# One decoder layer on one core: the output projection of the token mixer by seven half-size products instead of eight blocks

## The chip, the cores and the metric

One core of a Trainium2 chip. A core has a matrix engine (TensorE, PE in the profile, with its weight loads as PEld), three engines for elementwise work (VectorE or DVE, ScalarE or ACT, GpSimd or POOL), a queue engine for transfers (SyncE or SP), an on-chip memory SBUF, and eight PSUM banks of 128 x 512 fp32 in which matmuls add up. Every engine runs its own instructions in their order in the program; waits between engines are semaphores. The metric is the device time of one execution in microseconds (us), lower is better.

## The reference, cut to what matters

A layer is a gated linear attention (GLA) mixer and a gated feed-forward part with a convolution, each on an RMS-normed input and added to the residual x, and a last norm. x is 1024 tokens by 1024 features, fp32.

```python
def gla_mixer(x, w_in, w_alpha_up, b_alpha, out_norm, w_out):
    proj = x @ w_in
    q, k, v, r, a_low = jnp.split(proj, ...)
...
    _, o = lax.scan(step, state0, (qc, kc, vc, cum))    # 4 heads, chunks of 64 tokens
    o = rms_norm(o, out_norm.reshape(h, dv)).reshape(b, s, GLA_DV)
    return (o.astype(x.dtype) * jax.nn.silu(r)) @ w_out
...
def conv_ffn(x, w_up, conv_w, conv_b, w_down):
    u = x @ w_up                                        # 1024 -> 2 * 2816
    u = sum(u_pad[:, j:j + s] * conv_w[j] for j in range(CONV_WIDTH)) + conv_b
    gate, up = jnp.split(u, 2, axis=-1)
    return (jax.nn.silu(gate) * up) @ w_down
...
    x = x + mixer(rms_norm(x, norm1))
    x = x + conv_ffn(rms_norm(x, norm2), ...)
    return rms_norm(x, final_norm)
```

The change is in the last line of `gla_mixer`: g = norm(o) * silu(r), a 1024 x 1024 matrix, times `w_out`, 1024 x 1024.

## The kernel before, in words

Every fp32 product is made of three matmuls on numbers split in two (hi is the value cast to fp32r, lo is the rest): hi times hi, hi times lo, lo times hi (`mm3`, lines 96, 98, 100; `prod`, line 560). A split is an ACT cast (hi) and a DVE subtraction (lo): lines 86 and 87 for a unit of weights (128 x 1024), 517 and 518 for g, 618 and 619 for the normed x.

The stages, in the order of PE's work: the projections q, k, v and the GLA chain head by head (chain matmuls `s_ps`, `u_ps`, `o_ps`; DVE and ACT work between them, lines 425 to 465); then r, in two column halves c = 0, 1 of eight token blocks of 128 each (`r_ps`, 24 matmuls of 128 x 512 per block); after each block silu (`sr`), the gate product g (`og`, POOL line 505, DVE line 511), four transposes of g (`gt_ps`) and its split into the big tile T. The last head's GLA chain runs beside the first blocks of r. Then the output projection (`out_tok`, tile `o_ps2`, which the profile shows as `o_ps`): two column halves n of eight token blocks of 24 matmuls, added by DVE to x (tiles `x2a` for tokens 0 to 511 and `x2b` for the rest, line 580). During n = 1, `norm2(tok)` squares and norms each finished token block (ACT `x2n`, `junk`; POOL `rstd`; DVE line 589) and `feat(tok - 2)` transposes it (`t_ps`, 8 transposes), splits it into T and, for the second half of the tokens, forms the sums that the feed-forward part's Strassen scheme needs (`combine`: lines 600 to 603 on DVE, with POOL's `r` additions of line 552). Last come the first two (plain) feature blocks of the feed-forward part (`plain_mm`, tile `u_ps`) and then its Strassen products (`xb`, `yb`, `zb`).

A scheduler sets the order of instructions by its own estimate of time, except inside `manual_schedule(engines={ET.PE})`, where PE's order is that of the code (output projection's n = 1 and all that follows). PSUM banks come from pools that are opened and closed; a tile in a bank waits until the bank's former content has been read. In the kernel before, r's tiles (pool `pr`, two buffers) lie in two banks that the last head's v left early, and the GLA chain's pool `sm` stays open until the plain blocks.

Of the kernel before, what the change touches and what calls it, by code (L numbers as in the profile page):

```python
# [54 lines left out]
def gla_convffn_kernel(  # L55
# [34 lines left out]
    def unit(i):  # L90
        return split_unit(load_unit(i), nc.vector)
# [41 lines left out]
    t3_dram = dram.tile([P, NP2, HALF], F32, name="t3_dram")  # L133
    t4_dram = dram.tile([P, NP2, HALF], F32, name="t4_dram")
    f4_dram = dram.tile([P, 4, HALF], F32, name="f4_dram")

# [334 lines left out]
    pa_stack.close()  # L471
    pr_stack, r1_stack, r2_stack = ExitStack(), ExitStack(), ExitStack()
# [14 lines left out]
    def x2_row(tok):  # L487
        return x2h[tok // 4][:, tok % 4, :]

    def gidx(c, half):  # L490
        return (8 + 2 * half) if c == 0 else 2 * half

    for c in range(2):
        wr = [unit(U_R + 4 * c + j) for j in range(4)]
        for tok in range(NG):
            ps = pr.tile([P, HALF], F32, name="r_ps", tag="r")
# [17 lines left out]
            for vt in range(4):  # L514
                nc.tensor.transpose(out=gt_ps[:, vt, :], in_=og[:, vt * P:(vt + 1) * P], identity=ident)
            gi = gidx(c, half)
# [3 lines left out]
            if c == 1 and tok % 2:  # L520
                nc.gpsimd.dma_start(out=x2h[half][:, tok % 4 - 1:tok % 4 + 1, :],
                                    in_=xt[(tok - 1) * P:(tok + 1) * P, :].rearrange("(a p) d -> p a d", p=P))

# [23 lines left out]
    def ld(dst, src):  # L547
        nc.sync.dma_start(out=dst, in_=src)
        return dst
# [17 lines left out]
    XT1, XT3, XT4 = xop(0), xop(2), xop(8)  # L567

    def out_tok(n, tok, wo):
        ns = slice(n * HALF, (n + 1) * HALF)  # L570
        ps = pr.tile([P, HALF], F32, name="o_ps2", tag="r")
        half, cs = tok // 4, slice((tok % 4) * P, (tok % 4) * P + P)
        for vt in range(KT):
            whi, wlo = wo[vt // 2]
            wc = slice((vt % 2) * HALF, (vt % 2 + 1) * HALF)
            gi = gidx(vt // 4, half)
            mm3([ps], T[:, gi, vt % 4, cs], T[:, gi + 1, vt % 4, cs],
                [whi[:, wc]], [wlo[:, wc]], vt == 0, vt == KT - 1)
        xs = x2_row(tok)[:, ns]
        nc.vector.tensor_tensor(out=xs, in0=ps, in1=xs, op=ALU.add)  # L580

# [42 lines left out]

    wo = [unit(U_O + j) for j in range(4)]
    for tok in range(NG):
        out_tok(0, tok, wo)

    ps_f = [[[None] * 2 for _ in range(2)] for _ in range(NPLAIN)]
    w_f = [None] * NPLAIN  # L630

    def plain_mm(pool, f, j, n):
        ps = pool.tile([P, HALF], F32, name="u_ps", tag=f"b{2 * f + j}")
        ps_f[f][j][n] = ps
        for kh in range(2):
            prod(ps, w_f[f][j], kh, ((X11, X21), (X12, X22))[n][kh], kh == 0)

    with tc.manual_schedule(engines={ET.PE}):
        wo = [unit(U_O + 4 + j) for j in range(4)]
        for tok in range(NG):  # L640
            out_tok(1, tok, wo)
            norm2(tok)
            if tok >= 2:
                feat(tok - 2)
            if tok == 5:
# [3 lines left out]
        pr_stack.close()  # L649
        pA = ctx.enter_context(tc.tile_pool(name="pA", bufs=1, space=PSUM, reuse_waits="tile"))  # L650
# [6 lines left out]
        ps_stack.close()  # L657
# [25 lines left out]
    def y_tile(name):  # L683
        return up.tile([P, S], F32, name=name, tag="y", bufs=4)
# [38 lines left out]

    def plain_evac(f):
        ys = []
        for j in range(2):
            y = y_tile("y")
            for n in range(2):
                nc.scalar.copy(out=y[:, n * HALF:(n + 1) * HALF], in_=ps_f[f][j][n])
            ys.append(y)  # L730
        return ys
# [51 lines left out]
    with tc.manual_schedule(engines={ET.PE}):  # L783
        ys = [plain_evac(f) for f in range(NPLAIN)]

# [24 lines left out]
        pC = pC_stack.enter_context(tc.tile_pool(name="pC", bufs=1, space=PSUM, reuse_waits="tile"))  # L810
        if NPLAIN > 1:
            plain_end(0, ys[0])
        prev, wn = None, w_load(NPLAIN)
        for f in range(NPLAIN, NF + 1):
            p4, q3 = finish_products(prev) if prev else (
                lambda: None, lambda: plain_end(NPLAIN - 1, ys[-1]))
            if f == NF:
                break
            if f == NP2:
# [275 lines left out]
```

## Time and profile before

| | |
|---|---|
| three timed runs | 1074.22, 1074.61, 1074.73 us; median 1074.61 |
| profiled execution | 1075.29 us |
| its span, first to last instruction | 1073.5 us (1.8 us lie around it) |
| PE busy | 1062.3 us, 99% of the span, 5272 instructions |
| DVE busy | 709.8 us, 66% |
| ACT busy | 509.4 us, 47% |
| POOL busy | 293.5 us, 27% |
| granted clock of PE, mean | 0.999 of full speed |

The output projection's matmuls run from 335.9 to 428.5 us of the span, with the transposes of six token blocks among them.

### The profile page before, as it was taken

What the parts mean: (1) busy time and instruction counts of PE and PEld (TensorE: products, weight loads), DVE (VectorE), ACT (ScalarE), POOL (GpSimd) and SP (SyncE); (2) the same over time, 40 slices, a digit from 0 to 9 for tenths busy, and PEclk for the clock granted to TensorE, in tenths of its full rate; (3) what the DMA queues carried; (4) which work ended last, traced back from release to release, by engine and by line L of the source; (5) the groups of instructions that cost most, each with busy time, mean ns of one, the idle gap of its engine ahead of it and who ended that gap; (6) DMA issues with size and microseconds to landing.
All of it is one profiled execution on the core that took longest, in us unless ns stands there. A gap on an engine that the chain in (4) does not pass through costs nothing.

```text
span 1073.5 us, 14018 instructions
## 1 busy us (share of the span) xinstructions
PE 1062.3 (99%) x5272; PEld 900.1 (84%) x5272; DVE 709.8 (66%) x890; ACT 509.4 (47%) x788; POOL 293.5 (27%) x264
## 2 busy tenths in 40 slices
PE   9999999999999999999999999999999999999997
PEld 7889999998888888888888888888888888888885
DVE  4566757575524146949676776777677758997963
ACT  6654645453323035446454555454444445544453
POOL 0100010031531012244325233545554421200311
PEclk9999999999999999999999999999999999999999
DMA  9511111241623131144434344445644569966482
GB/s 338 212 60 50 66 55 48 78 168 48 202 65 118 49 108 40 51 158 175 176 118 157 118 169 145 108 127 151 152 110 127 133 172 338 387 234 192 158 267 81
DMA packets 64148, 153.26 MB, mean 143 GB/s; under 512 B 7248, under 2 KB 10064, under 8 KB 63568
## 3 DMA queue, kind: packets, MB, share of 16 engines
q1 hardware_dynamic: 55392, 130.08, 35.0%
q0 software_dynamic: 8688, 22.29, 8.7%
q8 instruction: 41, 0.67, 0.2%
q14 instruction: 27, 0.22, 0.1%
HBM read 106.99 MB, written 45.35 MB: 142 GB/s over the span
## 4 chain that ended last, share of the span: by engine, by line
PE 95%; DMA 3%; ACT 1%; DVE 1%; SPq 0%; issue 0%; POOLq 0%; POOL 0%; ACTq 0%
PE xb L560 20%; PE zb L560 10%; PE bw L763 8%; PE bx L763 6%; PE yb L560 5%; PE u_ps L560 4%; PE o_ps L96 3%; PE o_ps L100 3%; PE o_ps L98 3%; PE bz L763 3%; PE by L763 3%; PE r_ps L96 3%; PE r_ps L100 3%; PE r_ps L98 3%; PE v_ps L100 2%; PE v_ps L96 2%
## 5 line engine op out<-in xcount | busy, mean ns | idle before, releaser
L560 PE MATMUL xb<-T,whi 128*128 128x512 f32 x640 | 197.1, 389 | 0.4 <-ACT yg L829 0.4
L560 PEld LDWEIGHTS xb<-T,whi 128*128 128x128 f32 x640 | 120.0, 188 | 25.6 <-ACT yg L829 0.9
L560 PE MATMUL xb<-T,wlo 128*128 128x512 f32 x320 | 124.5, 389 | 0.0
L534 DVE TENSOR_TENSOR wlo<-s,whi 128x1024 fp32r<-128x1024 f32 x40 | 65.8, 1644 | 58.7 <-ACT whi L533 58.6
L560 PE MATMUL zb<-T,whi 128*128 128x512 f32 x320 | 98.5, 389 | 0.0
L552 POOL TENSOR_TENSOR s<-raw 128x512 f32<-128x512 f32 x40 | 56.9, 1426 | 139.1 <-DVE wlo L534 87.0
L560 PEld LDWEIGHTS xb<-T,wlo 128*128 128x128 f32 x320 | 60.1, 188 | 12.6
L560 PEld LDWEIGHTS zb<-T,whi 128*128 128x128 f32 x320 | 60.1, 188 | 12.5
L534 DVE TENSOR_TENSOR wlo<-raw,whi 128x1024 fp32r<-128x1024 f32 (+1 forms) x40 | 40.1, 1002 | 37.0 <-ACT whi L533 37.0
L560 PE MATMUL zb<-T,wlo 128*128 128x512 f32 x160 | 62.2, 389 | 0.0
L552 POOL TENSOR_TENSOR s<-s,raw 128x512 f32<-128x512 f32 x40 | 61.5, 1538 | 1.6
L467 POOL DMA_DIRECT2D o_dram<-o_sb x16 | 12.0, 749 | 178.4 <-DVE o_sb L462 121.4
L533 ACT CAST whi<-s 128x1024 fp32r<-128x1024 f32 x40 | 42.0, 1050 | 33.6 <-PE xb L560 27.0
L86 ACT CAST whi<-raw 128x1024 fp32r<-128x1024 f32 x32 | 33.6, 1051 | 50.5 <-PE o_ps L100 34.3
L533 ACT CAST whi<-raw 128x1024 fp32r<-128x1024 f32 (+1 forms) x40 | 33.3, 833 | 48.4 <-PE zb L560 30.2
L552 POOL TENSOR_TENSOR cv<-cv 128x512 f32<-128x512 f32 x12 | 26.5, 2209 | 108.5 <-DVE cv L709 108.5
L96 PE MATMUL v_ps<-whi,T 128*128 128x256 f32 x192 | 54.5, 284 | 0.0
L100 PE MATMUL v_ps<-whi,T 128*128 128x256 f32 x192 | 54.5, 284 | 0.0
L98 PE MATMUL v_ps<-wlo,T 128*128 128x256 f32 x192 | 54.4, 283 | 0.0
L763 PE MATMUL bw<-whi 128*128 128x512 f32 x132 | 51.5, 390 | 0.0
L763 PE MATMUL bw<-whi,wlo 128*128 128x512 f32 x132 | 51.4, 389 | 0.0
L763 PE MATMUL bw<-wlo,whi 128*128 128x512 f32 x132 | 51.3, 389 | 0.0
(286 smaller groups left out, 2924.2 us busy)
## 6 DMA issues: line engine op xcount, KB each, us to landing
raw<-in_w_dram SPq DMA_DIRECT2D x74, 512.0 KB, 3.6
t_dram<-cv SPq DMA_DIRECT2D x44, 256.0 KB, 2.5
t_dram<-cv POOLq DMA_DIRECT2D x33, 256.0 KB, 6.7
t<-in_w_dram SPq DMA_DIRECT2D x33, 256.0 KB, 3.9
t<-t_dram SPq DMA_DIRECT2D x33, 256.0 KB, 4.2
ab<-in_w_dram SPq DMA_DIRECT2D x32, 256.0 KB, 3.3
h_dram<-cv SPq DMA_DIRECT2D x12, 512.0 KB, 4.2
ab<-h_dram SPq DMA_DIRECT2D x21, 256.0 KB, 2.9
```

The source lines that it names most:

```text
L86: nc.scalar.copy(out=hi, in_=raw)
L96: nc.tensor.matmul(out=outs[j], lhsT=ah, rhs=bh[j], start=start, stop=False)
L98: nc.tensor.matmul(out=outs[j], lhsT=ah, rhs=bl[j], start=False, stop=False)
L100: nc.tensor.matmul(out=outs[j], lhsT=al, rhs=bh[j], start=False, stop=stop)
L467: nc.gpsimd.dma_start(out=o_dram[:, g - 1:g + 1, h * DV:(h + 1) * DV], in_=o_sb)
L533: nc.scalar.copy(out=dst_hi, in_=src)
L534: nc.vector.tensor_tensor(out=dst_lo, in0=src, in1=dst_hi.bitcast(F32), op=ALU.subtract)
L552: nc.gpsimd.tensor_tensor(out=out, in0=a, in1=b, op=op)
L560: nc.tensor.matmul(out=out, lhsT=a[:, ks], rhs=b[:, kt, :], start=start and kt == 0 and j == 0, stop=kt == 3 and j == 2, skip_group_check= ...
L763: nc.tensor.matmul(out=out, lhsT=a[:, ts], rhs=b[:, H1], start=start and j == 0, stop=stop and j == 2, skip_group_check=True)
```

## The change

With g and `w_out` cut into 2 x 2 blocks of 512 x 512 (in g the first index is the half of the tokens, the second the half of g's columns), the output is formed from seven products: g11 w11, g12 w21, g22 (w21 - w11 + w12 - w22 up to sign), and the four with sums S1 = g21 + g22, S2 = S1 - g11, S3 = g11 - g21, S4 = g12 - S2. Each product is four token blocks of 12 matmuls of 128 x 512: 7 x 4 x 12 = 336 matmuls where there were 8 x 2 x 24 = 384.

What is new or moved:

- `gates_in` takes the place of one split per r block. The sums of g are formed per token block in the tile of `x2b` (whose load of x comes later), with DVE additions (`vadd`) and more splits.
- `x2a` is loaded before r, `x2b` in two halves late in r's second column half, whose blocks run in the order 4, 5, 6, 7, 0, 1, 2, 3.
- The product g11 w11 (tile `ob`, four banks) stands between r's two column halves; the other six follow r, all in code order on PE.
- Sums of weight units: 20 loads of `w_out` units in place of 8, one of them written out (`tw_dram`) and read back, 8 DVE additions of 128 x 1024, 14 weight splits in place of 8.
- PSUM: `sm` closes with the last head. r's two buffers and the transposes' two lie in the banks of the pool `pa`, the `ob` banks in those of `sm`.
- `norm2` and `feat` stand beside the products S4 and g22; `feat(4)` to `feat(7)` among the plain blocks at n = 0. Entering the feed-forward part, ACT's order is that of the code, and the first plain block's convolution moves ahead.

```diff
@@ r and the sums of g
+    ps_stack.close()
-    pr = pr_stack.enter_context(tc.tile_pool(name="pr", bufs=2, space=PSUM, side="right"))
+    pr = pr_stack.enter_context(tc.tile_pool(name="pr", bufs=2, space=PSUM))
+    sm = pr_stack.enter_context(tc.tile_pool(name="smr", bufs=2, space=PSUM))
+    pc = pc_stack.enter_context(tc.tile_pool(name="pc", bufs=1, space=PSUM, side="right", reuse_waits="tile"))
...
+    def vadd(dst, a, b, op=ALU.add):
+        nc.vector.tensor_tensor(out=dst, in0=a, in1=b, op=op)
+
+    def gates_in(c, half, cs, ps):
...
+        a, b = a21[:, :, cs], s3[:, :, cs]
+        if c == 0 and half == 0:
+            split(col(G11), col(G11 + 1), ps)
+        elif c == 0:
+            nc.scalar.copy(out=a, in_=ps)
+            vadd(b, col(G11).bitcast(F32), ps, ALU.subtract)
+            vadd(b, col(G11 + 1).bitcast(F32), b)
+            split(col(S3), col(S3 + 1), b)
+        elif half == 1:
+            split(col(G22), col(G22 + 1), ps)
+            vadd(b, ps, b, ALU.subtract)
+            vadd(a, ps, a)
+            split(col(S2), col(S2 + 1), b)
+            split(col(S1), col(S1 + 1), a)
+        else:
+            split(col(G12), col(G12 + 1), ps)
+            vadd(b, ps, b, ALU.subtract)
+            split(col(S4), col(S4 + 1), b)
+
+    def gprod(ps, gi, w, t, start):
...
+    x2_load(0, 0, 4)
     for c in range(2):
+        if c:
+            w1 = [unit(U_O + j) for j in range(2)]
+            for t in range(4):
+                ob[t] = pc.tile([P, HALF], F32, name="ob", tag=f"o{t}")
+                gprod(ob[t], G11, w1, t, True)
+                x2_acc(0, t, H0, ob[t])
-        for tok in range(NG):
+        for tok in (range(NG), (4, 5, 6, 7, 0, 1, 2, 3))[c]:
...
-            nc.scalar.copy(out=T[:, gi, :, cs], in_=gt_ps)
-            nc.vector.tensor_tensor(out=T[:, gi + 1, :, cs], in0=gt_ps, in1=T[:, gi, :, cs].bitcast(F32),
-                                    op=ALU.subtract)
+            gates_in(c, half, cs, gt_ps)
@@ the products, norm2 and feat
     with tc.manual_schedule(engines={ET.PE}):
-        wo = [unit(U_O + 4 + j) for j in range(4)]
-        for tok in range(NG):
-            out_tok(1, tok, wo)
-            norm2(tok)
-            if tok >= 2:
-                feat(tok - 2)
...
+        for t in range(4):
+            ps = pr.tile([P, HALF], F32, name="o2", tag="r")
+            gprod(ps, G12, w2, t, True)
+            x2_acc(0, t, H0, ps)
+        for t in range(4):
+            gprod(ob[t], S2, w6, t, False)
+            x2_acc(1, t, H0, ob[t])
+        for t in range(4):
+            gprod(ob[t], S1, w5, t, False)
+            x2_acc(0, t, H1, ob[t])
+            x2_acc(1, t, H1, ob[t])
...
+        for t in range(4):
+            ps = pr.tile([P, HALF], F32, name="o2", tag="r")
+            gprod(ps, S3, w7, t, True)
...
+            b21, t2 = load_unit(U_O + 2 + j), ld(raw_tile("t2w"), tw_dram[:, j, :])
+            vadd(b21, b21, t2, ALU.subtract)
...
+        for t in range(4):
+            ps = pA.tile([P, HALF], F32, name="o3", tag=f"b{t}")
+            gprod(ps, S4, w3, t, True)
+            x2_acc(0, t, H1, ps)
+            norm2(t)
+            if t >= 2:
+                feat(t - 2)
+        for t in range(4):
+            ps = pA.tile([P, HALF], F32, name="o4", tag=f"b{t}")
+            gprod(ps, G22, w4, t, True)
+            x2_acc(1, t, H0, ps)
+            norm2(4 + t)
+            if t < 2:
+                feat(2 + t)
...
             for j in range(2):
-                plain_mm(pA, f, j, 0)
-                if j == 0:
-                    feat(6 + f)
+                for kh in range(2):
+                    plain_mm(pA, f, j, 0, (kh,))
+                    if kh == f:
+                        feat(4 + 2 * f + j)
```

How the change moves instructions, at three places. First PE's order where r begins, beside the last head's chain (`s_ps`, `u_ps` and `o_ps` are the chain's matmuls, `r_ps` the first block of r; the numbers are buffers). Before:

```order
L100 MATMUL u_ps_2489<-T_66,kT_620 128x256 [waits DVE_49]
L96 MATMUL s_ps_2499<-T_66 128x128 [waits PE_49]
L98 MATMUL s_ps_2499<-T_66 128x128
L100 MATMUL s_ps_2499<-T_66 128x128
L96 MATMUL r_ps_2752<-whi_2730,T_66 128x512 [waits DVE_49]
L98 MATMUL r_ps_2752<-wlo_2731,T_66 128x512
```

And now:

```order
L100 MATMUL o_ps_2566<-shi_2523,T_66 128x256
L96 MATMUL s_ps_2587<-T_66 128x128 [waits DVE_49]
L98 MATMUL s_ps_2587<-T_66 128x128
L100 MATMUL s_ps_2587<-T_66 128x128
L96 MATMUL r_ps_2761<-whi_2739,T_66 128x512 [waits DVE_49,PE_49]
L98 MATMUL r_ps_2761<-wlo_2740,T_66 128x512
```

Before, r's first block follows the chain's second `s_ps`; now it follows the fifth, behind 24 more chain matmuls of 128 x 256 and 9 of 128 x 128 (33 in all). Its bank is now one that the last head's second v tile (`v_ps_2375`) still holds.

Second, DVE at the same time. `v_ps_2374` before and `v_ps_2375` now are that v tile, and line 245 (246 now) reads it out, one head chunk of 128 tokens each time. Before, from the last weight split to the last two read-outs (the row with x2):

```order
L87 TENSOR_TENSOR wlo_3067<-raw_3064,whi_3066 128x1024 [waits DMAHW5_49,Activation_49]
L429 TENSOR_TENSOR scl_2486<-sc_f0_616,sch_2485 128x128 [waits Activation_49]
L245 SCALAR_TENSOR_TENSOR T_66<-v_ps_2374,rstd_1_83,T_66 128x256 [waits Activation_49]
L445 SCALAR_TENSOR_TENSOR slo_2496<-U_2493,cg_2230,shi_2495 128x256 [waits Activation_49]
L429 TENSOR_TENSOR scl_2505<-sc_f1_618,sch_2504 128x128 [waits Activation_49]
L245 SCALAR_TENSOR_TENSOR T_66<-v_ps_2374,rstd_1_83,T_66 128x256 [waits Activation_49] x2
```

Now, from behind `scl_2506` (the same place as `scl_2505`) to the last read-out:

```order
L426 COPY_PREDICATED sc_f0_617<-mask_70,s_ps_2527 128x128 [waits DVE_49,PE_49]
L463 COPY o_sb_2513<-o_ps_2509 128x256 [waits DMASW2_49,PE_49]
L246 SCALAR_TENSOR_TENSOR T_66<-v_ps_2375,rstd_1_83,T_66 128x256 [waits Activation_49]
L446 SCALAR_TENSOR_TENSOR slo_2524<-U_2521,cg_2231,shi_2523 128x256 [waits Activation_49]
L440 SCALAR_TENSOR_TENSOR U_2551<-U_2521,cg_2231,u_ps_2547 128x256 [waits DVE_49,PE_49]
L430 TENSOR_TENSOR scl_2533<-sc_f0_617,sch_2532 128x128 [waits Activation_49]
L463 COPY o_sb_2513<-o_ps_2536 128x256 [waits PE_49]
L426 COPY_PREDICATED sc_f1_619<-mask_70,s_ps_2557 128x128 [waits PE_49]
L246 SCALAR_TENSOR_TENSOR T_66<-v_ps_2375,rstd_1_83,T_66 128x256 [waits Activation_49]
```

Seven operations of the chain now stand among and ahead of the last two read-outs (an eighth, `U_2521`, has moved ahead of `slo_2497`); before there were none.

Third, PE where the last token block's transposes end and the plain blocks' second half (n = 1) begins. Before, the transposes are followed by a product of the first half, here its first row, and n = 1 starts 24 matmuls later at the row with buffer 4251:

```order
L616 MATMUL t_ps_4198<-ident_69,x2b_2718 128x128 [waits DVE_49,PE_49]
L616 MATMUL t_ps_4198<-ident_69,x2b_2718 128x128 x3
L560 MATMUL u_ps_4222<-T_66,whi_4162 128x512 [waits Activation_49]
...
L560 MATMUL u_ps_4251<-T_66,whi_4063 128x512 [waits DVE_49,Activation_49]
L560 MATMUL u_ps_4251<-T_66,whi_4063 128x512
```

Now n = 1 (buffer 4341) follows at once:

```order
L657 MATMUL t_ps_4313<-ident_69,x2b_2726 128x128 [waits DVE_49,PE_49]
L657 MATMUL t_ps_4313<-ident_69,x2b_2726 128x128 x3
L614 MATMUL u_ps_4341<-T_66,whi_4091 128x512 [waits DVE_49,Activation_49]
L614 MATMUL u_ps_4341<-T_66,whi_4091 128x512 [waits DVE_49]
```

The product that stood between the last transposes and the first matmul that needs their split is gone from there.

## Rows read from the trace of the kernel before

**Rows 1.** The page, busy time, share of the span and instructions.

```profile
PE 1062.3 (99%) x5272; PEld 900.1 (84%) x5272; DVE 709.8 (66%) x890; ACT 509.4 (47%) x788; POOL 293.5 (27%) x264
```

**Rows 2.** Windows: stretch, us; busy PE, PEld, DVE, ACT, POOL; PEclk, DMA share, GB/s.

```profile
231.00:240.00 9.00, 9.00 (x56) 8.00 (x55) 7.96 (x17) 5.18 (x13) 1.38 (x2) 1.00 0.70 271
240.00:290.00 50.00, 50.00 (x268) 42.74 (x268) 25.36 (x51) 20.37 (x43) 18.29 (x21) 1.00 0.31 105
...
429.00:447.00 18.00, 18.00 (x89) 15.06 (x88) 17.88 (x25) 7.85 (x15) 7.44 (x6) 1.00 0.15 45
```

**Rows 3.** Chain that ended last, in the output projection: start, length, what.

```profile
403.20 0.87 PE t_ps L616 x8
409.54 0.87 PE t_ps L616 x8
```

**Rows 4.** Timeline of PE where r begins: start, us, instruction.

```profile
231.58 0.22 PE L96 MATMUL s_ps<-T 128*128 128x128 f32 x1
...
232.56 0.44 PE L96 MATMUL r_ps<-whi,T 128*128 128x512 f32 x1
...
237.38 0.39 PE L100 MATMUL r_ps<-whi,T 128*128 128x512 f32 x1
237.61 0.28 PE L96 MATMUL o_ps<-T,sch 128*128 128x256 f32 x1
```

**Rows 5.** Timeline of DVE there; in brackets the idle time before and its releaser.

```profile
231.42 2.05 DVE L87 TENSOR_TENSOR wlo<-raw,whi 128x1024 fp32r<-128x1024 f32 x1 [2.87 <-ACT whi L86]
...
234.52 1.21 DVE L87 TENSOR_TENSOR wlo<-raw,whi 128x1024 fp32r<-128x1024 f32 x1
...
237.89 0.48 DVE L245 SCALAR_TENSOR_TENSOR T<-v_ps,rstd,T 128x256 fp32r<-128x256 f32 x1 [0.54 <-ACT T L244]
238.40 0.48 DVE L439 SCALAR_TENSOR_TENSOR U<-U,cg,u_ps 128x256 f32<-128x256 f32 x1
238.80 0.30 DVE L425 COPY_PREDICATED sc_f<-mask,s_ps 128x128 f32<-128x128 int32 x1
239.00 0.42 DVE L462 COPY o_sb<-o_ps 128x256 f32<-128x256 f32 x1
239.46 0.49 DVE L445 SCALAR_TENSOR_TENSOR slo<-U,cg,shi 128x256 fp32r<-128x256 f32 x1
```

**Rows 6.** Groups by line and form, 228 to 500 us: busy us, mean ns.

```profile
L87 DVE TENSOR_TENSOR wlo<-raw,whi 128x1024 fp32r<-128x1024 f32 x17 | 22.9, 1359 | 6.4 <-ACT whi L86 5.9
...
L589 DVE SCALAR_TENSOR_TENSOR x2a<-x2a,rstd,n2b 128x1024 f32<-128x1024 f32 x4 | 7.2, 1793 | 5.9 <-POOL rstd L126 5.9
L589 DVE SCALAR_TENSOR_TENSOR x2b<-x2b,rstd,n2b 128x1024 f32<-128x1024 f32 x4 | 6.1, 1534 | 0.1
...
L709 DVE TENSOR_TENSOR h<-ca,cv 128x1024 f32<-128x1024 f32 x2 | 2.4, 1224 | 0.2 <-ACT ca L708 0.2
...
L618 ACT CAST T<-t_ps 128x512 fp32r<-128x512 f32 x16 | 9.0, 585 | 18.2 <-PE t_ps L616 18.2
```

**Rows 7.** Timelines of DVE and POOL at one token's norm.

```profile
394.86 1.29 DVE L589 SCALAR_TENSOR_TENSOR x2a<-x2a,rstd,n2b 128x1024 f32<-128x1024 f32 x1 [2.71 <-POOL rstd L126]
...
403.24 0.69 DVE L580 TENSOR_TENSOR x2a<-o_ps,x2a 128x512 f32<-128x512 f32 x1
...
407.31 2.30 DVE L589 SCALAR_TENSOR_TENSOR x2a<-x2a,rstd,n2b 128x1024 f32<-128x1024 f32 x1 [0.27 <-POOL rstd L126]
...
407.24 1.29 POOL L552 TENSOR_TENSOR r<-T 128x512 f32<-128x512 f32 x1
```

**Rows 8.** Timeline of DVE, one token with its sums to the next.

```profile
442.59 0.68 DVE L619 TENSOR_TENSOR T<-t_ps,T 128x512 fp32r<-128x512 f32 x1
...
448.28 0.68 DVE L619 TENSOR_TENSOR T<-t_ps,T 128x512 fp32r<-128x512 f32 x1
```

**Rows 9.** Waits of PE from 225 to 490 us, all of them.

```profile
PE xb L560 <- ACT yg L829: 0.4, 1, 0.4
```

**Rows 10.** Windows at the end of the span, columns as in rows 2.

```profile
1068.00:1070.00 2.00, 0.00 (x0) 0.00 (x0) 0.95 (x2) 1.14 (x2) 0.88 (x2) 1.00 0.50 184
1070.00:1072.00 2.00, 0.00 (x0) 0.00 (x0) 0.00 (x0) 0.00 (x0) 0.00 (x0) 0.77 0.94 348
1072.00:1073.50 1.50, 0.00 (x0) 0.00 (x0) 0.00 (x0) 0.00 (x0) 0.00 (x0) 0.50 0.01 1
```

More of the change, by code (lines that the diff above doesn't have):

```diff
@@ L134, in gla_convffn_kernel @@
     t4_dram = dram.tile([P, NP2, HALF], F32, name="t4_dram")
+    tw_dram = dram.tile([P, 2, D], F32, name="tw_dram")
     f4_dram = dram.tile([P, 4, HALF], F32, name="f4_dram")
@@ L488, in x2_row, with x2_load @@
         return x2h[tok // 4][:, tok % 4, :]
-    def gidx(c, half):
-        return (8 + 2 * half) if c == 0 else 2 * half
-    for c in range(2):
+    def x2_load(half, a, b):
+        nc.gpsimd.dma_start(out=x2h[half][:, a:b, :],
+                            in_=xt[(4 * half + a) * P:(4 * half + b) * P, :].rearrange("(a p) d -> p a d", p=P))
+    a21, s3 = (x2h[1][:, 2 * i:2 * i + 2, :].rearrange("p a (b t) -> p (a b) t", b=2) for i in range(2))
+    G11, G12, G22, S1, S2, S3, S4 = 8, 0, 8, 4, 6, 10, 2
@@ new lines, in gprod @@
+    def gprod(ps, gi, w, t, start):
+        cs = slice(t * P, (t + 1) * P)
+        for kt in range(4):
+            whi, wlo = w[kt // 2]
+            wc = slice((kt % 2) * HALF, (kt % 2 + 1) * HALF)
+            gh, gl = T[:, gi, kt, cs], T[:, gi + 1, kt, cs]
+            for j, (a, b) in enumerate(((gh, whi), (gh, wlo), (gl, whi))):
+                nc.tensor.matmul(out=ps, lhsT=a, rhs=b[:, wc], start=start and kt == 0 and j == 0,
+                                 stop=kt == 3 and j == 2, skip_group_check=True)
@@ L567, in gla_convffn_kernel @@
     XT1, XT3, XT4 = xop(0), xop(2), xop(8)
[L569 to L580, printed above, removed]
     def norm2(tok):
@@ new lines, in gla_convffn_kernel @@
+    with tc.manual_schedule(engines={ET.PE}):
+        w2 = [unit(U_O + 2 + j) for j in range(2)]
+        w6, w5 = [], []
+        for j in range(2):
+            b12, b11, b22 = (load_unit(U_O + i + j) for i in (4, 0, 6))
+            vadd(b12, b12, b11, ALU.subtract)
+            vadd(b22, b22, b12, ALU.subtract)
+            nc.sync.dma_start(out=tw_dram[:, j, :], in_=b22)
+            w6.append(split_unit(b22, nc.vector))
+            w5.append(split_unit(b12, nc.vector))
+        for t in range(4):
[9 more added lines that the diff above has]
+            x2_acc(1, t, H1, ob[t])
+        pc_stack.close()
+        pA = ctx.enter_context(tc.tile_pool(name="pA", bufs=1, space=PSUM, side="right", reuse_waits="tile"))
+        w7 = []
+        for j in range(2):
+            b22, b12 = (load_unit(U_O + i + j) for i in (6, 4))
+            vadd(b22, b22, b12, ALU.subtract)
+            w7.append(split_unit(b22, nc.vector))
+        for t in range(4):
+            ps = pr.tile([P, HALF], F32, name="o2", tag="r")
+            gprod(ps, S3, w7, t, True)
+            xs = x2h[1][:, t, :].rearrange("p (a d) -> p a d", a=2)
+            vadd(xs, ps.unsqueeze(1).broadcast_to([P, 2, HALF]), xs)
+        w3 = [unit(U_O + 6 + j) for j in range(2)]
+        w4 = []
+        for j in range(2):
+            b21, t2 = load_unit(U_O + 2 + j), ld(raw_tile("t2w"), tw_dram[:, j, :])
+            vadd(b21, b21, t2, ALU.subtract)
+            w4.append(split_unit(b21, nc.vector))
+        pr_stack.close()
+        sm = sm_stack.enter_context(tc.tile_pool(name="smt", bufs=4, space=PSUM, reuse_waits="tile"))
+        for t in range(4):
[12 more added lines that the diff above has]
+                feat(2 + t)
+            if t == 1:
@@ L783, in gla_convffn_kernel @@
     with tc.manual_schedule(engines={ET.PE}):
-        ys = [plain_evac(f) for f in range(NPLAIN)]
+        act = ExitStack()
+        act.enter_context(tc.manual_schedule(engines={ET.Activation}))
+        y0, y1 = plain_evac(0, 0), plain_evac(1, 0)
+        plain_evac(0, 1, y0)
+        c0 = [conv(0, j, y0[j]) for j in range(2)]
+        gate(0, c0[0], c0[1], c0[0])
         def finish_products(st):
```

66 lines of the change are left out of this document (32 added, 34 removed).

## The prediction

> **What bounds the kernel now.** I read the page first: PE is busy 1062.3 of 1073.5 us [rows 1], so only PE work taken out, or PE time left empty, moves the end. Then the windows over the stretch that the change touches: PE is busy for the whole of each of them at the granted clock 1.00, which is 2.4 GHz [rows 2]. The list of PE's waits confirms it: from 225 to 490 us there is one, of 0.4 us, at the entry of the feed-forward part [rows 9]. So the removed matmuls are paid back in full, and every wait that the change brings is a loss in full. The second thing that the windows show is DVE: it has half its time free while r runs (25.36 of 50 us), but 17.88 of 18 us are taken while the normed tokens' sums are made (429 to 447 us) [rows 2]. The new code has less PE work there for DVE to hide behind.
>
> **What is removed.** 384 matmuls become 336, all of 128 x 512. The chain gives their price: from the end of one token's transposes (403.20 + 0.87 = 404.07) to the start of the next (409.54) lie exactly the 24 matmuls of one output block, 5.47 us, 0.228 each [rows 3]. 48 x 0.228 = **10.9 us less**. Transposes, r, chain and plain matmuls stay the same in number.
>
> **What is added beside PE.** The sums of g are 16 DVE additions and 16 more splits, 32 DVE operations of 128 x 512 at 0.63 us (nine such from 442.59 to 448.28 [rows 8]), 20 us over both halves of r. DVE has about half of that stage free [rows 2], so I cost them at nothing; without that cover they would cost what exceeds it. Six more weight splits (1.36 each) and eight additions of 128 x 1024 (nearest row 1.22) [rows 6] are another 18 us, spread over r and 44 us of products; they too are hidden on average, but not at the places below, where a wait in DVE's order stands ahead of something PE needs.
>
> **Loss 1, where r begins: 4.0 us.** Before, PE has done nine chain matmuls from 231.58 to 232.56, then r fills the time in which DVE and ACT work on the chain, up to 237.61 [rows 4]. Now r's first matmul waits for the last read-out of the last v tile, and PE's order puts 33 more chain matmuls ahead of it. When does that read-out end? Before, at 237.89 + 0.48 = 238.37, after DVE had stood still for 0.54 [rows 5]. Now eight chain operations stand ahead of it that came later before: two U updates (0.48), two predicated copies (0.30), two o copies (0.42), one slo (0.49), one scl (near 0.30): 3.2 us of durations, 2.5 from start to start, since each starts before the former's end (238.40, 238.80, 239.00, 239.46). 238.37 - 0.54 + 2.5 = 240.3. From 231.58 to 240.3 are 8.7 us; PE's work there is the nine matmuls (0.98) and the 33, at the 0.11 to 0.12 of these nine 3.7: 4.7 us. The rest, 4.0, is empty. Behind it nothing is won back, since PE has no idle time to give. Bounds: if the split that took 2.05 us here takes 1.21 like its neighbour [rows 5], 3.2; if each of the some eight hops between engines adds 0.2, near 6.
>
> **Loss 2, weights and x in DVE's order: 1.2 us (0 to 2).** The o2 products have two PSUM buffers, so PE's third block waits for DVE's addition of the first. For S3 there stand between the last matmul of S1 and that addition two weight splits (1.13 from start to start), four additions (0.63) and the 128 x 1024 one itself (1.22): 6.0 us, against two blocks of 12 matmuls, 5.46. With the vadd that waits for `tw_dram`'s read ahead of them I take 0.9; for g12 w21, whose last block stands behind a vadd of loaded weights, 0.3. Below nothing is excluded.
>
> **Loss 3, norm2 to feat: 1.2 us (0 to 2.5).** Before, a token's feat came two output blocks (10.9 us) after its own; now two of 2.73 us. In the trace the way from the addition to the end of the norm is 403.24 to 407.31 + 2.30 = 409.61, 6.4 us, or 5.4 where the last step takes 1.29 [rows 7]. `feat(0)` has 5.46 us, `feat(1)` 6.3 (a transpose group more), `feat(2)` and `feat(3)` 7.2, but those two stand behind the splits of the first and of two weight units on DVE. I take 0.2 and 1.0. The whole stretch from S4 to n = 1 gives DVE little air: PE has 192 matmuls and 64 transposes, 43.7 + 7.0 = 50.7 us; DVE has 4 weight splits (4.5), 8 additions and 16 splits of 0.63 (15.1), 8 norms (10.3) and 4 tokens' sums, 28 operations (17.6): 47.5, and 50.5 if three norms take 1 us longer, as the means 1793 and 1534 ns say of before [rows 6].
>
> The 2.30 is a norm that began 0.06 us after a POOL addition of 1.29 [rows 7]: the two add up. The Trainium skill, page "SBUF — State Buffer", section "SBUF: two separate sides", says why: VectorE and GpSimd share a port pair, locked for a whole instruction when VectorE reads two SBUF inputs. Here the trace agrees. By that rule each of the 12 norms and weight splits that meets an addition costs up to 1.29 more; by the rows three do, and the sum above stands.
>
> **Loss 4, n = 1 right behind the last transposes: 0.65 us (0.6 to 1.9).** Its second matmul needs the lo of token 7. Before, 5.46 us of another product lay between. Now: half the transposes end 0.43 before the end of the group, then ACT 0.585 [rows 6], then DVE 0.68 [rows 8]: 0.83 after the last transpose, less the first matmul's 0.23: 0.6 empty. It is more where DVE is late with token 6's sums: nine operations, 5.7 us [rows 8], against 5.46 + 0.87 of PE, so it keeps up.
>
> At the entry of the feed-forward part the 0.4 of before [rows 9] may go or stay; ACT's new order moves the convolution ahead of it. I take no change (0.4 less to 1.0 more).
>
> **The sum.** -10.9 + 4.0 + 1.2 + 1.2 + 0.65 = -3.85. The profiled execution took 1075.29 us, of which 1.8 lie around the span; 1071.4 for such a one. It was 0.7 above the median of 1074.61, so the forecast for the median is **1070.8 us**.
>
> **Rivals.** *Only loss 1 and 4 are real* (chance 0.2): DVE has air in r, gets ahead on weights, and norms that miss POOL's additions end in 5.4 us. Then -10.9 + 3.2 to 4.0 + 0.6: about 1067.4 to 1068.0. Against it speaks the 47.5 of 50.7.
>
> *Nothing is lost* (0.05): the order in which r stands behind v's read-out costs nothing. Then 1063.7. The 5.05 us of r between 232.56 and 237.61 [rows 4] speak against: they filled just this wait.
>
> *DVE becomes the bound from S4 to n = 1* (0.33, half of it within 0.2% of before): slower from the point where DVE's surplus passes the 3.85 gained. If all 12 norms and weight splits meet a POOL addition, DVE needs 47.5 + 12 = 59.5 of 50.7 us; 8.8 empty in place of 1.85 makes -3.85 + 6.95 = +3.1: 1077.7. For it: a saturated DVE in rows 2; against it: three of eight met one before. If half meet, 1073 to 1075, no change.
>
> *The clock falls where r begins* (0.02): for 8.7 us PE would be half empty, in pieces of 1 to 2 us. In the trace the clock fell to 0.50, 1.2 GHz, only in 1072.00 to 1073.50, after two windows without any PE instruction, the first still at 1.00 [rows 10]. Each matmul at half the clock costs 0.228 more; 17 of them undo the gain, 34 make it 1074.6 + 3.9 = 1078.5. The Trainium skill, page "TensorE: Matmul & The Clock Gate", section "HAM oscillation — how this bites in real kernels", describes matmul groups with waits between them that lose the clock again and again; no stretch of this trace has that.
>
> **How the numbers follow.** What a measurement of this kernel tells from no change is about 0.2%, 2.1 us: faster means below 1072.5, slower above 1076.8. My own sum (losses of 5.5 to 8.5 us, 1069 to 1072.4) has 0.4, the first two rivals 0.25, DVE's case 0.33, the clock 0.02. Faster: 0.4 and 0.25, less a little for sums at the edge, 0.63; the same 0.2; slower 0.17. To hold eight in ten I leave out the rival without loss and the worst half of the slower cases: **1066.5 to 1076.5**; the likeliest case alone has 1069 to 1072.4.
>
> **What would show it.** Right: PE has about 5224 matmul instructions; between the end of v and r's first matmul PE is busy for under 5 of 9 us, and r's first matmul has the last v read-out on DVE as its releaser; PE's waits name DVE lines 504, 511 and 630 (the splits, sums and norm) with about 3 us in all between S1 and n = 1; the feed-forward part is as long as before. Wrong: r's first matmul near 232.6; PE waits in r itself, which would mean that the sums of g are not hidden; a DMA (`tw_dram`, the late `x2b`) as releaser with more than 1 us; a clock below 1.00 in any window before 1060 us; or a norm in which POOL's additions meet every DVE step.

## The result: slower by 0.7%, and the profile after

The changed kernel takes 1081.66 us (median of six runs, 1079.23 to 1083.09) against 1074.17 of the kernel before on the same chip: ratio 1.0067, 95% interval 1.0054 to 1.0080. The forecast was 1070.8 with a range to 1076.5. Its runs lie 3.9 us apart, those of before 0.7 (1074.00 to 1074.73), and the longer ones have the lower mean clock: 1079.23 us at 0.996 of full speed, 1083.09 at 0.993.

Four views of the profiled execution (1081.92 us, span 1080.1) tell where the time went. The page first, for [rows 1]:

```profile
PE 1057.3 (98%) x5224; PEld 893.0 (83%) x5224; DVE 761.3 (70%) x952; ACT 526.1 (49%) x809; POOL 303.7 (28%) x263
```

The 48 matmuls are gone (5272 to 5224), worth 10.9 us, but PE's busy time fell by 5.0 only. So not only idle time was added; some matmuls took longer. Idle time rose from 11.2 to 22.8 us, by 11.6, and the work took 5.9 more than the removal alone would leave: 17.5 us added where the sum had 7.05. Second, PE's waits from 225 us to the end, for [rows 9] (total, times, longest); before there was one line of 0.4 in this stretch:

```profile
PE xb L614 <- DVE wlo L504: 3.2, 1, 3.2
PE t_ps L657 <- DVE x2a L630: 2.3, 1, 2.3
PE xb L614 <- ACT whi L503: 1.7, 1, 1.7
...
PE o L543 <- DVE x2b L511: 0.9, 1, 0.9
...
PE o_ps L96 <- ACT sch L429: 0.7, 1, 0.7
PE u_ps L96 <- DVE U L440: 0.6, 2, 0.4
PE o_ps L100 <- DVE scl L430: 0.3, 1, 0.3
PE u_ps L614 <- ACT T L659: 0.2, 1, 0.2
PE u_ps L614 <- DVE T L660: 0.2, 1, 0.2
```

Two lines stand at the entry of the feed-forward part (`xb`), 4.9 us together: the place where I had taken no change. `t_ps` is the fourth feat, `o` the product with S3, `o_ps` and the `u_ps` of L96 the chain where r begins, the `u_ps` of L614 the plain blocks' second halves. Third, the windows around these waits (columns as in [rows 2]):

```profile
231.00:237.00 6.00, 4.62 (x34) 3.90 (x32) 5.95 (x15) 4.08 (x12) 0.00 (x0) 1.00 0.47 157
237.00:243.00 6.00, 5.81 (x24) 4.88 (x24) 4.18 (x14) 2.77 (x11) 0.77 (x1) 0.72 0.17 61
...
414.00:418.00 4.00, 2.33 (x11) 1.60 (x9) 4.00 (x6) 2.58 (x5) 3.83 (x5) 1.00 0.36 133
418.00:422.00 4.00, 3.36 (x13) 3.01 (x14) 4.00 (x6) 2.23 (x5) 1.09 (x2) 0.62 0.38 137
...
478.00:482.00 4.00, 1.37 (x3) 1.17 (x4) 4.00 (x4) 2.90 (x5) 0.36 (x1) 0.80 0.90 317
482.00:486.00 4.00, 4.00 (x15) 3.14 (x14) 2.59 (x3) 1.46 (x3) 0.00 (x0) 0.78 1.00 307
```

The third number from the right is what I had given 2 in 100: PEclk at 0.72, 0.62 and 0.78 to 0.80, a clock at half speed (1.2 GHz) for part of the window, three times, each time behind a wait. The loss is at most (1 - 0.72) x 6 = 1.7 us at r's start, 0.38 x 4 = 1.5 behind the fourth feat (0.2 more in the 2 us after), and (0.20 + 0.22) x 4 = 1.7 at the entry; a part of each falls into the wait itself. Fourth, the timelines of DVE, ACT and POOL at the entry:

```profile
465.85 2.48 DVE L783 SCALAR_TENSOR_TENSOR cv<-y,vec_sb,cv 128x1023 f32<-128x1023 f32 x2 [8.00 <-ACT cv L782]
468.24 4.54 DVE L785 SCALAR_TENSOR_TENSOR cv<-y,vec_sb,cv 128x1022 f32<-128x1022 f32 x2
472.89 2.13 DVE L793 TENSOR_TENSOR cv<-cv 128x1024 f32<-128x1024 f32 x1
474.94 4.50 DVE L504 TENSOR_TENSOR T<-t,T 128x1024 fp32r<-128x1024 f32 x2
479.36 1.21 DVE L504 TENSOR_TENSOR wlo<-raw,whi 128x1024 fp32r<-128x1024 f32 x1
...
475.59 1.03 ACT L503 CAST whi<-raw 128x1024 fp32r<-128x1024 f32 x1
...
467.36 4.34 POOL L606 TENSOR_TENSOR s<-raw 128x512 f32<-128x512 f32 x2 [21.10 <-DMA raw<-in_w_dram]
471.67 4.47 POOL L606 TENSOR_TENSOR s<-s,raw 128x512 f32<-128x512 f32 x2
```

Read it from PE's side: the first product of the feed-forward part waits for a cast of its weights (475.59) and then for their split (479.36). ACT's new order puts the convolution of the first plain block ahead of that cast, and DVE follows: 465.85 to 475.0 convolution and gate, then two splits of the sums `T`, then those of the weights. And the convolution takes longer than it would alone: its steps read two SBUF operands, and while POOL makes its four sums (467.36 to 476.1) two of them take 4.54 where the first two took 2.48, as the 2.30 in [rows 7]. POOL pays as well: two sums in 4.34 and 4.47 us.

### The profile page after: what moved, and what is told of

Its sections match the earlier page's. It is cut to its first block, busy times and chain, and to the rows that moved or that the text cites. A ratio compares the mean times of both kernels' runs of the same rounds, so it can differ in the third digit from the quotient of the medians.

```text
span 1080.1 us, 14042 instructions
## 1 busy us (share of the span) xinstructions
PE 1057.3 (98%) x5224; PEld 893.0 (83%) x5224; DVE 761.3 (70%) x952; ACT 526.1 (49%) x809; POOL 303.7 (28%) x263
## 4 chain that ended last, share of the span: by engine, by line
PE 89%; DVE 4%; DMA 4%; ACT 1%; issue 1%; SPq 0%; POOLq 0%; POOL 0%; DVEq 0%; ACTq 0%
PE xb L614 20%; PE zb L614 10%; PE bw L844 8%; PE bx L844 6%; PE yb L614 5%; PE u_ps L614 3%; PE bz L844 3%; PE by L844 3%; PE r_ps L96 3%; PE r_ps L98 3%; PE r_ps L100 3%; PE o L543 2%; PE v_ps L100 2%; PE v_ps L98 2%; PE v_ps L96 2%; PE qk_ps L96 2%
## 5 line engine op out<-in xcount | busy, mean ns | idle before, releaser
L614 PE MATMUL xb<-T,whi 128*128 128x512 f32 x640 | 198.0, 391 | 1.7 <-ACT whi L503 1.7
L614 PEld LDWEIGHTS xb<-T,whi 128*128 128x128 f32 x640 | 120.8, 189 | 27.2 <-ACT whi L503 2.2
L614 PE MATMUL xb<-T,wlo 128*128 128x512 f32 x320 | 125.3, 392 | 3.2 <-DVE wlo L504 3.2
L606 POOL TENSOR_TENSOR s<-raw 128x512 f32<-128x512 f32 x40 | 59.2, 1483 | 147.2 <-DVE wlo L504 82.6
L614 PE MATMUL zb<-T,whi 128*128 128x512 f32 x320 | 98.5, 389 | 0.0
L614 PEld LDWEIGHTS xb<-T,wlo 128*128 128x128 f32 x320 | 60.5, 189 | 16.2 <-DVE wlo L504 3.7
L614 PEld LDWEIGHTS zb<-T,whi 128*128 128x128 f32 x320 | 60.1, 188 | 12.4
L606 POOL TENSOR_TENSOR s<-s,raw 128x512 f32<-128x512 f32 x40 | 64.3, 1608 | 1.5
L614 PE MATMUL zb<-T,wlo 128*128 128x512 f32 x160 | 62.3, 389 | 0.0
L86 ACT CAST whi<-raw 128x1024 fp32r<-128x1024 f32 x38 | 39.8, 1051 | 44.0 <-PE ob L543 18.7
L606 POOL TENSOR_TENSOR cv<-cv 128x512 f32<-128x512 f32 x13 | 28.8, 2213 | 105.9 <-DVE cv L793 105.9
L96 PE MATMUL v_ps<-whi,T 128*128 128x256 f32 x192 | 54.5, 284 | 0.0
L87 DVE TENSOR_TENSOR wlo<-raw,whi 128x1024 fp32r<-128x1024 f32 x38 | 47.7, 1261 | 6.7 <-ACT whi L86 5.9
```

The lines of the kernel that those rows point to most:

```text
L86: nc.scalar.copy(out=hi, in_=raw)
L87: eng.tensor_tensor(out=lo, in0=raw, in1=hi.bitcast(F32), op=ALU.subtract)
L96: nc.tensor.matmul(out=outs[j], lhsT=ah, rhs=bh[j], start=start, stop=False)
L606: nc.gpsimd.tensor_tensor(out=out, in0=a, in1=b, op=op)
L614: nc.tensor.matmul(out=out, lhsT=a[:, ks], rhs=b[:, kt, :], start=start and kt == 0 and j == 0, stop=kt == 3 and j == 2, skip_group_check= ...
```

## The experiments

All are timed beside the kernel before on the same chip; a ratio is to that one. One to four share a chip, and so do five to eight. The medians of the kernel before that stand beside the versions lie between 1074.17 and 1074.94 us, so a difference between versions from two chips can be off by up to 0.8.

### One: the entry as before

```diff
-        act = ExitStack()
-        act.enter_context(tc.manual_schedule(engines={ET.Activation}))
-        y0, y1 = plain_evac(0, 0), plain_evac(1, 0)
-        plain_evac(0, 1, y0)
-        c0 = [conv(0, j, y0[j]) for j in range(2)]
-        gate(0, c0[0], c0[1], c0[0])
+        ys = [plain_evac(f) for f in range(NPLAIN)]
...
+        if NPLAIN > 1:
+            plain_end(0, ys[0])
```

> The changed kernel with the entry of the feed-forward part as it was before (ACT's order left to the scheduler, the first plain block's convolution in PSUM and behind the preparation of the first Strassen weights); all else of the change stays. Theory 'entry': the convolution moved ahead of the weight casts and splits made PE wait some 5.4 us there, and the clock that fell behind it cost 1.6 more; so about 7 us less than the changed kernel, near 1075, still not faster than before by the 10.9 us of the removed matmuls because of the losses at r's start, S3 and the feats. Rival 'lateness': the sums and weights arrive late because everything ahead of the entry got tighter, and the wait only moves; then within 2 us of the changed kernel.

Measured: 1077.36 us (1075.95 to 1079.28, nine runs), 1.0026 [1.0016, 1.0036]: 4.3 less than the changed kernel, not 7, and still slower than before. Both theories get a part. The two waits for casts and splits are gone, but another has come to the same place:

```profile
PE xb L614 <- ACT yg L913: 3.3, 1, 3.3
```

It is the wait of [rows 9], 0.4 before. A candidate for its cause is the queue that loads the weights, here SP's and POOL's timelines of this run:

```profile
455.65 0.80 SPq L602 DMA_DIRECT2D t<-f_dram  x2
456.50 25.08 SPq L80 DMA_DIRECT2D raw<-in_w_dram  x7
...
463.64 3.22 POOL L606 TENSOR_TENSOR s<-raw 128x512 f32<-128x512 f32 x2 [21.11 <-DMA raw<-in_w_dram]
```

The weights of the first Strassen block are loaded behind the reads of the last sums (`t`), which wait until the last token's sums are written. From there on loads, POOL's sums, casts and convolution take their time whatever PE does. In the kernel before, 5.46 us of a product lay between the last feat and the plain blocks' second halves; now those follow at once, so PE reaches the entry earlier than this chain. Experiments six and seven test both.

In this profiled execution the clock stayed at 1.00 where r begins, with the same waits as in the changed kernel:

```profile
231.00:237.00 6.00, 4.61 (x29) 3.57 (x28) 6.00 (x16) 4.33 (x12) 0.00 (x0) 1.00 0.57 175
237.00:243.00 6.00, 5.83 (x32) 5.05 (x32) 3.48 (x12) 2.23 (x8) 0.77 (x1) 1.00 0.12 44
```

### Two: the new entry alone, on the kernel before

The edit is that of experiment one the other way round, on the kernel before.

> The kernel before, with nothing but the new entry of the feed-forward part (ACT in code order, first plain block's convolution ahead of the weights' preparation, in SBUF). Theory 'entry': slower than before by 5 to 7 us, 1079 to 1081. Rival 'lateness': the new entry costs nothing where the stages ahead of it are as before, 1074 to 1075.

1079.33 us (1077.21 to 1079.70, five runs), 1.0039 [1.0027, 1.0052]: 4.8 us slower than the kernel before, a little under the expectation. PE has two new waits from 225 to 560 us, and no other in place of them:

```profile
PE xb L560 <- DVE wlo L534: 1.8, 1, 1.8
PE xb L560 <- ACT whi L533: 1.3, 1, 1.3
```

So the new entry costs by itself, with no Strassen in the output projection. Behind these waits the clock is at 0.59 from 478 to 482 us.

The edit moves two things at once, the convolution's place in the order and its sums' place in memory (SBUF in place of PSUM), and no run separates them. The durations allow an estimate. Here is DVE up to the first split of weights in this run:

```profile
465.21 3.60 DVE L699 SCALAR_TENSOR_TENSOR cv<-y,vec_sb,cv 128x1023 f32<-128x1023 f32 x2 [11.88 <-ACT cv L698]
468.74 3.49 DVE L701 SCALAR_TENSOR_TENSOR cv<-y,vec_sb,cv 128x1022 f32<-128x1022 f32 x2
472.33 1.23 DVE L709 TENSOR_TENSOR cv<-cv 128x1024 f32<-128x1024 f32 x1
473.48 3.43 DVE L534 TENSOR_TENSOR T<-t,T 128x1024 fp32r<-128x1024 f32 x2
476.83 1.21 DVE L534 TENSOR_TENSOR wlo<-raw,whi 128x1024 fp32r<-128x1024 f32 x1
```

The splits of `T` in the kernel before:

```profile
472.35 2.36 DVE L534 TENSOR_TENSOR T<-t,T 128x1024 fp32r<-128x1024 f32 x2
```

And a convolution step of experiment one, whose sums lie in PSUM, with POOL's additions beside it:

```profile
476.52 1.29 DVE L783 SCALAR_TENSOR_TENSOR ca<-y,vec_sb,ca 128x1023 f32<-128x1023 f32 x1 [0.37 <-ACT ca L782]
...
476.13 2.50 POOL L606 TENSOR_TENSOR s<-raw 128x512 f32<-128x512 f32 x2 [6.64 <-DMA raw<-in_w_dram]
```

At 2.48 for two steps and 2.36 for the splits of `T`, these operations took 1.1, 1.0 and 1.1 us longer than alone: 3.2, and PE's two waits are 3.1. In the changed kernel the later two steps, the gate product and the splits of `T` took 2.1, 0.9 and 2.1 longer: 5.1, and the waits are 4.9. So by this estimate the meeting with POOL is nearly all of the wait, and the new order alone would have cost little; a run with the new order and the sums in PSUM would decide it.

### Three: r's buffers in the early banks

```diff
-    pr = pr_stack.enter_context(tc.tile_pool(name="pr", bufs=2, space=PSUM))
     sm = pr_stack.enter_context(tc.tile_pool(name="smr", bufs=2, space=PSUM))
+    pr = pr_stack.enter_context(tc.tile_pool(name="pr", bufs=2, space=PSUM))
```

> The changed kernel with the two PSUM pools of r and of its transposes opened in the other order, so that r's two buffers lie in the banks of the last head's first v tile, which was read out early, and the transposes take those of the second. Theory 'r's start': r fills the wait of the last head's chain again, PE has no wait and no lower clock from 231 to 243 us; 5.0 us less (3.7 of waits, 1.3 of clock), near 1076.7. Rival: the first transposes of g, now in the late banks, or the order around them take the wait over; then within 1.5 us of the changed kernel.

1076.73 us (1074.82 to 1080.05, eleven runs), 1.0021 [1.0012, 1.0031]: 4.9 less than the changed kernel. r's first matmul follows nine chain matmuls again, and the 5.0 forecast for it are met. The windows have no idle time and no lower clock:

```profile
231.00:237.00 6.00, 6.00 (x34) 5.13 (x32) 4.74 (x12) 3.03 (x7) 0.00 (x0) 1.00 0.49 175
237.00:243.00 6.00, 6.00 (x39) 5.37 (x39) 3.71 (x10) 3.81 (x9) 0.77 (x1) 1.00 0.12 44
```

### Four: PE kept busy in the entry's wait

```diff
+            if f == NPLAIN:
+                for _ in range(14):
+                    nc.tensor.matmul(out=xb, lhsT=g1[0][:, 0:P], rhs=X11[0][:, 0, :], start=True, stop=True,
+                                     skip_group_check=True)
             prod(xb, g1, 0, X11, True)
```

> The changed kernel with 14 more matmuls on PE at the feed-forward part's entry, repeats of the first one of the first product, which that one then overwrites (it starts the sum anew); 3.2 us of PE time in a wait of 3.5 us. Theory 'clock': the wait is as long as before, but PE is not idle in it, the granted clock stays at 1.00 from 478 to 486 us, and 1.5 us are won: near 1080. Rival: the clock does not depend on PE's idling there, it falls all the same, and the time is the changed kernel's or, where the repeats push the following matmuls back, up to 3 us more.

1078.89 us (1078.33 to 1081.20, five runs), 1.0046 [1.0034, 1.0059]: with 3.2 us more PE work 2.8 us less than the changed kernel. The 14 repeats lie in the wait; of the profiled execution's windows there, none is below 1.00:

```profile
474.00:478.00 4.00, 3.97 (x18) 2.94 (x17) 4.00 (x3) 2.83 (x6) 1.01 (x1) 1.00 0.76 258
478.00:482.00 4.00, 4.00 (x20) 3.29 (x19) 3.63 (x5) 2.54 (x3) 0.00 (x0) 1.00 0.99 320
482.00:486.00 4.00, 4.00 (x19) 3.33 (x18) 2.44 (x3) 1.37 (x2) 2.44 (x2) 1.00 0.53 213
```

One execution does not show that this is because PE was kept busy: in the same one the clock also stayed at 1.00 where r begins and behind the fourth feat's wait of 2.2 us, where nothing was filled. All traces together say more. At the entry the clock fell in the five executions that left PE waiting for 2.9 us or more (4.9 in the changed kernel and in three, 3.3 in one, 3.1 in two, 2.9 in five), and in none of the other five: this one, and six to nine with waits of 1.0 to 1.8. The gain is 2.8 us by the medians and 1.8 by the means, which five runs do not tell from the 1.5 expected; the clock also stays up elsewhere in some of them (mean 0.999 at 1078.33, 0.995 at 1081.20).

### Five to eight: both repairs, then earlier loads and earlier feats

Five has both repairs (experiments one and three). Six adds the loads, seven the feats, eight both:

```diff
@@ six: loads ahead of the reads of the last sums
+        wn = w_load(NPLAIN)
         for a in range(2):
             r = ld(raw_tile("t4").rearrange("p (k t) -> p k t", k=2), f4_dram[:, 2 * a:2 * a + 2, :])
@@ seven: the last four feats earlier
             for j in range(2):
-                for kh in range(2):
-                    plain_mm(pA, f, j, 0, (kh,))
-                    if kh == f:
-                        feat(4 + 2 * f + j)
+                feat(4 + 2 * f + j)
+                plain_mm(pA, f, j, 0)
```

> Both repairs: the entry of the feed-forward part as before, and r's buffers in the banks that are free early. If the two losses are separate, their gains add: 1081.7 less 4.3 less 4.9, near 1072.5, about 2 us under the kernel before. Rival: what is won at r's start is given back at the entry, where the chain of sums, weight loads and convolution now ends last (the first run with the old entry waited 3.3 us for ACT there, the kernel before 0.4); since everything ahead of the last feat comes earlier with it, that wait should keep its length. If the rival is right, then 1075 to 1077.

> As the kernel with both repairs, but the two weight loads of the first Strassen block stand in SP's queue ahead of the reads of the last sums (which wait until the last token's sums are written), not behind them. Theory 'queue': the loads land some 6 us earlier, POOL's sums and ACT's casts with them, and the wait of 3.3 us at the entry goes, with the lower clock behind it: 3 to 4 us less than with both repairs, 1069 to 1070. Rival: the loads are not what ends last there, DVE's and ACT's order is; then the same within 1 us.

> As the kernel with both repairs, but the last four feats stand one plain half or whole product earlier, so that a whole product (5.46 us) lies between the last one and the second halves, as in the kernel before. Theory 'spacing': the losses of 0.5 us at the start of the second halves and of up to 3.3 us at the entry go, because the chain from the last sums to the entry has 5.46 us more of PE work over it: 3 to 4 us less than with both repairs, 1069 to 1070. Rival: DVE is the bound in the stretch from S4 on, its norms and sums do not come earlier, and PE waits at the feats in place of the entry; then no gain, within 1 us.

> Earlier weight loads and earlier feats together, on the kernel with both repairs. If either takes the whole wait at the entry, both together win no more than the better of them, but for the 0.5 us at the start of the second halves: near 1069. If each takes a part, the sum of both: the remaining losses are then about 1 us at S3 and 2.3 at the fourth feat, and 1074.5 less 10.9 plus 3.3 makes 1067.

| | median (runs), us | ratio to before | wait at the entry |
|---|---|---|---|
| five, both repairs | 1073.92 (11) | 0.9992 [0.9983, 1.0000] | 2.9 |
| six, and loads | 1071.91 (6) | 0.9969 [0.9958, 0.9981] | 1.0 |
| seven, and feats | 1069.34 (5) | 0.9956 [0.9942, 0.9969] | 1.8 |
| eight, and both | 1069.62 (5) | 0.9952 [0.9940, 0.9965] | 1.0 |

Five lies between its theory and its rival: of the 4.9 won at r's start 3.4 remain on top of the old entry, and the wait at the entry stays (2.9 after 3.3). Six: the queue was part of the cause, 2.0 us and not 3 to 4, though in its profiled execution the clock fell behind the fourth feat (0.57 from 416 to 420 us) and not at the entry; seven: the spacing was the larger part, 4.6, with the 0.4 at the second halves gone as well. Eight is seven within what the runs can tell: the wait is as short as in six, but in its profiled execution the clock fell behind the fourth feat (0.72 from 412 to 418 us), in that of seven it did not. Eight's time is that of its first case, near 1069; the 1067 of the other is not reached, but with the clock's falls between them the runs do not decide. The rival of seven, a wait that moves to the feats, did not come: the fourth feat waits 2.3 us in five, seven and eight and 2.6 in six, after 2.3 in the changed kernel.

### Nine: the first four feats one block later

```diff
-            if t >= 2:
-                feat(t - 2)
+            if t == 3:
+                feat(0)
...
-            if t < 2:
-                feat(2 + t)
-            if t == 1:
+            if t < 3:
+                feat(1 + t)
+            if t == 2:
```

> As the kernel with both repairs, earlier loads and earlier last feats, but the first four feats each stand one block of 12 matmuls (2.73 us) later on PE. The fourth feat has waited 2.3 us for its norm on DVE in every run so far, with two weight splits and the POOL collisions ahead of it, and in some executions the clock fell behind that wait. Theory 'too near': one block more covers it; the 2.3 us and the clock go, about 3 us less than without it: near 1066.5. Rival 'DVE is full': the work that DVE does from S4 to the second halves is what bounds, and the wait moves to one of the last four feats or to the second halves; then within 1 us of 1069.6.

1067.17 us (1066.21 to 1068.84, five runs), 0.9932 [0.9918, 0.9945]: 2.4 less than eight, and 7.8 less than the kernel before. The wait went and did not move; all of PE's waits from 225 to 560 us are now

```profile
PE xb L614 <- ACT yg L912: 1.0, 1, 1.0
PE o L543 <- DVE x2b L511: 0.5, 1, 0.5
PE u_ps L614 <- DVE T L660: 0.4, 1, 0.4
```

This is the fastest version, ahead of both kernels. It keeps the seven products and the sums of g as they are in the change; only places have been moved.

## Why the prediction was wrong, by its own steps

**The step that failed** is the entry of the feed-forward part: "I take no change (0.4 less to 1.0 more)". It cost 4.3 us (experiment one) to 4.8 (two), clock included. I had read that the convolution moves ahead of the weights' preparation and did not add up what then stands ahead of the first split on DVE: four convolution steps and a gate product, 6.3 us by the durations of the profile (4 x 1.28 and 1.22), the splits of `T`, 2.36, and what POOL's sums beside them add. By the estimate in experiment two this last term, 5.1 us, is nearly the whole wait of 4.9; it is not separated by a run. That POOL and DVE hold each other up I had used for the norms, by the rows of one norm, and not for the one place where these steps meet four POOL sums. The Trainium skill, page "SBUF — State Buffer", section "SBUF: two separate sides", has a VectorE instruction with two SBUF inputs contend with a GpSimd instruction that reads SBUF; the 4.54 here in place of 2.48, and the 1.29 with one input in PSUM, agree with it. And loss 4 was worked out only to the first matmul: the product no longer between the last feat and the second halves was also cover for the loads and sums at the entry. That is the 3.3 us that stayed in experiment one.

**The second** is the chance of the clock's fall, 2 in 100. I argued that no stretch of the trace had a clock below 1.00 with PE at work; but no stretch of it had waits like these either, so the trace of before could not speak against it. It fell three times in the profiled execution, at 1.5 to 1.7 us each at most, and its mean differs from run to run. The Trainium skill, page "TensorE: Matmul & The Clock Gate", section "HAM oscillation — how this bites in real kernels", describes matmul groups with waits between them that lose the clock every time. The runs agree in that the clock fell behind waits; but the page's example has longer ones, and here a wait of 2.3 us, or a group of which none is over 0.7, lost the clock in some executions and not in others.

**Removed work**, 10.9 us: nothing in the runs speaks against it. With nearly all waits taken out, nine lies 7.8 below before, and its three waits of 1.9 us against the 0.4 of [rows 9] are 1.5 of the missing 3.1. I have not traced the rest. In its profiled execution, 9.1 below that of before, PE's busy time is 11.9 less (1050.4), so all of the 10.9 is there, and every window up to 1056 us, just ahead of the end of PE's work, has the clock at 1.00.

**Loss 1**, 4.0 forecast: experiment three won 4.9, five over one 3.4. The mechanism is half as predicted. The banks decide, since exchanging them took the loss away; but r's first matmul has no wait of its own for the read-out. In both traces it follows the chain's last matmul at once, in the changed kernel at 239.97, 1.0 after the read-out's end (238.95). What cost time are the 33 chain matmuls that the order had put ahead of it, which wait for ACT and DVE. In the run of experiment one, where the clock held, r's first matmul came 7.9 us after the chain's first (230.53 to 238.42), with the last read-out of v ending at 238.27; the forecast was 8.7. The weight split that took 2.05 in [rows 5] took 1.23 there, which was the lower bound's case: 7.9 less 4.7 of work are the 3.2 of that bound. The fall of the clock makes up for the difference in the changed kernel.

**Loss 2**, 1.2 forecast: the wait for x's addition at S3 is 0.9 as written; the g12 product loses about 0.5 in the trace by the spacing of its matmuls, 0.3 forecast. **Loss 3**, 1.2 forecast: 2.3 for the fourth feat alone, and the clock behind it; experiment nine won 2.4. Where it went, DVE's timeline in the changed kernel shows:

```profile
410.75 0.68 DVE L511 TENSOR_TENSOR x2a<-o,x2a 128x512 f32<-128x512 f32 x1
411.36 2.85 DVE L87 TENSOR_TENSOR wlo<-raw,whi 128x1024 fp32r<-128x1024 f32 x2
414.13 1.28 DVE L660 TENSOR_TENSOR T<-t_ps,T 128x512 fp32r<-128x512 f32 x2
...
416.52 1.97 DVE L630 SCALAR_TENSOR_TENSOR x2a<-x2a,rstd,n2b 128x1024 f32<-128x1024 f32 x1
```

Between the token's addition and its norm stand the two weight splits that I had named, three splits of normed tokens and another addition; 410.75 to 418.49 are 7.7 us, against the 7.2 that PE had work for. And DVE came to the addition late: PE's wait began at 416.2, so the matmuls before that addition had ended 7.2 earlier, at 409.0, 1.8 before it began. **Loss 4**, 0.65: two waits of 0.2 and the first matmuls' spacing, 0.9 in all.

**The rival that DVE becomes the bound from S4 to the second halves** did not happen: PE is at work for all of 424 to 448 us, and in nine, where DVE is busy for all of this stretch (24.00 of 24 us), PE's one wait there is 0.4. Of all my cases its 1077.7 lies next to the result but for the clock's, and for another reason. Its milder form was summed wrongly: half of the meetings make 53.5 of 50.7 us, which gives 1071.7 and not 1073 to 1075; and "only loss 1 and 4" reaches to 1068.3. The sums of g are hidden, as costed: no wait in r from 243 to 355 us. They are 20 additions and 12 more splits, not 16 and 16; the 32 in all are right.

## What to carry to other kernels

Work moved ahead on an engine has to be priced against everything in that engine's order that it now stands before, and with the other engine that it meets there, and the cover that a moved product gave must be looked for to the end of the chain behind it, not only at its first consumer. PE time that waits leave open can cost more than itself, since the clock may fall behind them: a wait in a kernel without waits is worth more than its length. The arithmetic saved by Strassen's scheme here (10.9 us) was real, and 7.8 of it came back only after r's PSUM banks, the entry, the weight loads and the place of eight feats were set anew.

## What the runs showed of the hardware that was not expected

The clock fell after short waits, and not in every execution. Where r begins in the changed kernel, PE had 4.62 us of work in 6 us, with no wait named longer than 0.7; the next 6 us had a mean clock of 0.72. In experiment one the same stretch had 4.61 in 6 us, and the next window 1.00. After one wait of 2.2 to 2.6 us at the fourth feat the clock fell in three profiled executions (0.62 in the changed kernel, 0.57 in six, 0.72 in eight) and in five not (1.00 in one, three, four, five and seven). So a single profile of a kernel with such waits shows one draw of several.

When DVE with two SBUF operands and POOL meet, both pay: two of POOL's additions took 4.34 and 4.47 us (3.24 and 2.66 for the same two pairs before), while two of DVE's convolution steps took 4.54 in place of 2.48. With one of the two operands in PSUM a step took 1.28 to 1.29 beside POOL's additions (experiment one).
